# Attention values in plain float32 on two halves of the array, one burst per pair of units

## The chip, the core and the metric

The kernel runs on one core of a Trainium2 chip. The core has five engines that work through queues of their own, in order: TensorE (matmuls, written PE; its weight loads are written PEld), VectorE (DVE), ScalarE (ACT), GpSimd (POOL) and SyncE (SP, which issues most transfers). Matmuls write into PSUM, eight banks of 128 partitions by 2 KB; the other data lies in SBUF. The metric is the device time of the whole kernel in microseconds, as the median of several runs. Beside it there is one profiled execution, from which all rows in this document come; an instruction of the kernel is named there by its line (L1235).

## What is computed

One layer of a hybrid attention block for 128 prompt tokens (tile 0) and 1024 latent tokens (tiles 1 to 8 of 128 tokens), in float32. A modulated RMS norm is followed by one input projection, then by two groups of attention heads, each with 8 query heads, 2 key/value heads and 64 columns a head, by a SiLU gate, and by one output projection.

```python
def global_attn_latent(q, k_lat, v_lat, k_ctx, v_ctx):           # mixer A
    ...
        s = jnp.einsum('bqkgd,bskd->bkgqs', qblk, k_all).astype(jnp.float32) * (d ** -0.5)
        p = jax.nn.softmax(s, axis=-1).astype(v_all.dtype)
        return jnp.einsum('bkgqs,bskd->bqkgd', p, v_all)

def window_attn_latent(q, k_lat, v_lat, k_ctx, v_ctx, sink):     # mixer B
    ...
    s = jnp.concatenate([sink_column(sink, kv, s_ctx.shape[:-1]), s_ctx, s_band], axis=-1)
    p = jax.nn.softmax(s, axis=-1).astype(v_lat.dtype)
    ...

def merge_out(o_a, g_a, o_b, g_b, w_out):
    return jnp.concatenate([o_a * jax.nn.silu(g_a), o_b * jax.nn.silu(g_b)], axis=-1) @ w_out
```

Mixer A attends to all 1024 latent keys and 128 context keys, nine blocks of 128 keys. Mixer B attends to the context block and to a band of at most three latent blocks. The prompt tile attends to its own block alone.

## The kernel before, in words

Up to about 302 us the kernel makes the modulated activations, the queries, keys, values and gates. The change touches there only how V is put away. The rest is the attention part, and this document is about it.

**Units, slots and pairs.** A *unit* is one token tile, one mixer (`m` = 0 for A, 1 for B) and one key/value head, with its four query heads side by side as 512 columns. The units run in pairs: a unit of A, then the unit of B of the same tile and head. Latent units come first (32, in 16 pairs), then the prompt's four. A unit consists of *slots*, one for each block of keys: nine for A; four for B, three in the first and the last tile; a prompt unit has one slot and an empty one. So a pair has mostly 13 slots, which are numbered 0 to 12 here.

**A slot.** The main loop at the end of `hybrid_step` goes over all slots. Each round first calls `tick()`, which runs what was put off with `later(n, f)` to this round. Then come, in this order, `scores` of the slot, the maxima and mixer-B scores that are due (`due`), some output products from the list `outq`, and `values` of the slot that was `LAG` = 3 rounds earlier. `in_order` then fixes this order on every engine, so that a waiting instruction holds up all that was written after it on the same engine.

- `scores`, mixer A: two products give the transposed scores of 128 keys by 512 queries in a PSUM bank `st` (tag B, two banks). The second of them (L1218) brings in the shift by the row's maximum, through `qb`. ACT makes the exponential `pe` (L1220) and casts it to the reduced format (`ph`, L1221). GpSimd subtracts to get the remainder `pl` (L1225), in one block of nine DVE does (L1223).
- `scores`, mixer B: four transposes of weights that are computed with the queries as rows (`penat`, L1212), then `ph` and `pl` in the same way by ACT (L1213) and DVE (L1214).
- `values`: V is stored as `v_hi` (its reduced format, 64 columns, and 64 more columns that are ones for A and V's remainder for B) and `v_lo`. Products L1235 (`ph`), L1237 (`v_lo`, A only) and L1238 (`pl`) add up 64 rows of values and, for A, 64 rows that all hold the sum of the exponentials, in a bank `pv` (tag C, two banks).
- The end of a unit, put off by the numbers in `END_AT`, counted from its last `values`: `inverse` (ACT takes the inverse sum as the exponential of a negative logarithm, or copies the second 64 rows for B), `gated` (DVE, two halves, L1259; GpSimd multiplies by the gate `sgl`, L1261; `load_gate` fetches the gate of a unit further on), `parts` (ACT casts to `ogh`, L1271; GpSimd subtracts to get `ogl`, L1274, one round later) and, after a unit of B, 24 output products appended to `outq` (L1313). They are taken from there at 2.5 a round. The first two products use `ogh` of the pair's A unit, the third `ogl` of it.

**What runs beside it.** In slots 0 to 3 of a pair the mixer-B scores `sn` (L998, L999) are made; DVE takes their maximum (L1002), and ACT their exponential one round later (L988). In slot 4 `finish` puts `ex` on GpSimd (L1020), and two rounds later `sum` (L1034). The inverse of these sums goes through a transpose and two transfers, and GpSimd multiplies it into the B gate (L1045). The maxima of a later A unit (L941, read by DVE at L942) stand in slots 4, 5, 7 and 8 (seven of them) and 9 to 12 (five, of which two in slot 11). After the last one they are turned (`ptm`, L960, in slot 12), and DVE writes them into `qb` (L961), which the next pair's slot 0 reads. At the end of a tile's output products DVE does two operations on each half of 512 columns (L1318, L1319).

**Elsewhere.** `modulate_rows` (L375) and `gate_rows` (L651) use plain float32 products with weights of 32 columns, on quarters of the array beside each other.

Of the kernel before, what the change touches and what calls it, by code (L numbers as in the profile page):

```python
# [18 lines left out]
P = 128  # L19
# [17 lines left out]
LAG = 3  # L37
# [41 lines left out]
PES = 3  # L79
GATE_LATE = 2  # L80
END_AT = (1, 4, 6, 9)
PROMPT_END = (2, 4, 5, 7)
# [48 lines left out]
def hybrid_step(ctx, tc, x_prompt, x_sample, cache_k_a, cache_v_a, cache_k_b, cache_v_b,  # L131
# [631 lines left out]
    v_hi = kv.tile([P, 2, 20, 2, HD], F32R, name="v_hi")  # L763
    v_lo = kv.tile([P, 20, HD], F32R, name="v_lo")
# [7 lines left out]
    def split_values(src, j):  # L772

        nc.vector.tensor_tensor(v_lo[:, j : j + 2, :], src[:, 0], v_hi[:, 0, j : j + 2, 0, :], op=ALU.subtract)
        nc.vector.tensor_tensor(v_hi[:, 1, j : j + 2, 1, :], src[:, 1], v_hi[:, 1, j : j + 2, 0, :], op=ALU.subtract)

    with tc.tile_pool(name="kt", bufs=2) as kt:
        W_GB.pools[WRAW : WRAW + 2] = [(kt, 2)] * 2
        sg_tile.append(lambda n: kt.tile([P, 512], F32, tag="kh", name=n))
        for b in range(0, 20, 4):  # L780
            later(4 + b // 2, lambda b=b: nc.gpsimd.tensor_scalar(
                v_hi[:, 0, b : b + 4, 1, :], gain4, 0.0, 1.0, op0=ALU.mult, op1=ALU.add))
        ones = ident_r.bitcast(F32)[64:68].unsqueeze(1)
        for out, n in ((kla[64:68].rearrange("p g b n -> p (g b) n"), 18), (klp[64:68, 0:2], 2)):
            later(ONES_AT, lambda out=out, n=n: nc.vector.tensor_scalar(
                out, ones.to_broadcast([4, n, P]), 0.0, 1.0, op0=ALU.mult, op1=ALU.add))
# [94 lines left out]
        later(VC_AT, lambda: nc.scalar.copy(v_hi[:, :, 0:2, 0, :], vc))  # L881
        later(VC_AT + 1, lambda: split_values(vc, 0))
# [295 lines left out]
    def blocks(t, m, g):  # L1178

        if t == 0:  # L1180
            k = (khp[:, g, :], klp[0:68, g, :]) if m == 0 else 0
            return [(k, v_hi[:, m, 18 + g], v_lo[:, 18 + g, :])]
        if m == 0:
            return [((kha[:, g, b, :], kla[:, g, b, :]), v_hi[:, 0, 2 * b + g], v_lo[:, 2 * b + g, :]) for b in range(9)]
        p0, p1_ = window(t)
        at = {p: b + 1 for b, p in enumerate(POS)}
        return [(p - p0, v_hi[:, 1, 2 * at.get(p, 0) + g], None) for p in range(p0, p1_)]
# [5 lines left out]
    def load_gate(i):  # L1193
        if i < NU:
            t, m, g = units[i]
            sgl[i] = w2.tile([P, 2, P], F32, tag="sgl", name=f"sgl{i}")
# [4 lines left out]
    def parts_tiles(i, b):  # L1201
        return [w3.tile([P, 512], F32R, tag=n, name=f"{n}{i}_{b}") for n in ("ph", "pl")]

    def scores(i, b, blk):
# [3 lines left out]
        ph, pl = parts_tiles(i, b)  # L1208
        if m == 1:
# [9 lines left out]
        pe = w3.tile([P, 512], F32, tag="pe", name=f"pe{i}_{b}", bufs=PES)  # L1219
        nc.scalar.activation(pe, s, AF.Exp)  # L1220
        nc.scalar.copy(ph, pe)  # L1221
        if (i - PROMPT_AT in PROMPT_PL) if t == 0 else b in PL_DVE:
            later(1, lambda: nc.vector.tensor_tensor(pl, pe, ph, op=ALU.subtract))  # L1223
        else:
            nc.gpsimd.tensor_tensor(pl, pe, ph, op=ALU.subtract)  # L1225
        return ph, pl

    def values(i, b, last, blk, ph, pl):
        t, m, g = units[i]
        _, vh, vl = blk  # L1230
        if b == 0:
            pvb[i] = bank(PROMPT_PV[i - PROMPT_AT] if t == 0 else "C", f"pv{i}")
        pv = pvb[i]
        two = vh.rearrange("p s d -> p (s d)")
        nc.tensor.matmul(pv, two, ph, start=(b == 0), stop=False)  # L1235
        if m == 0:
            nc.tensor.matmul(pv[0:64, :], vl, ph, start=False, stop=False)  # L1237
        nc.tensor.matmul(pv, two, pl, start=False, stop=last)  # L1238
        if not last:
            return  # L1240
# [210 lines left out]
```

## Time and profile before

| | |
|---|---|
| runs, lowest / median / highest | 704.09 / 704.34 / 704.47 us |
| profiled execution, its span | 704.1 us |
| first score product of the attention part (L1217) | 301.85 us |
| transfers | 78.64 MB, mean 112 GB/s |

The page of the profile gives each engine's busy time and its share of the span, then groups of instructions as "line, engine, operation, written tile <- read tiles, shape, xcount | busy us, mean ns of one | idle us of the engine ahead of them, and what ended it". Lines of the order of time begin with start and duration in us. A line of the windows view has the stretch and its length, then the busy time of PE, PEld, DVE, ACT and POOL with their instruction counts, TensorE's granted clock, the share of the transfer engines and GB/s. `[0.43 <-PE st L1218]` says that the engine stood idle for 0.43 us until PE's write of `st` at that line. TensorE's clock is granted in full for nearly the whole span.

### The profile page before, as it was taken

The numbers are of one execution on the slowest core, as the hardware profiler recorded it, in microseconds if no ns is written. First come the engines' busy times: TensorE is split into PE (matmuls) and PEld (weight loads), VectorE is DVE, ScalarE is ACT, GpSimd is POOL, SyncE is SP. The second block draws the span as 40 slices with busy tenths as digits, with TensorE's granted clock in tenths as the row PEclk, the third lists the DMA queues.
The fourth block names the chain that finished last, engine by engine and source line by source line (L and its number), as shares of the span: only waits on it lengthen the run. The fifth ranks groups of instructions, "written<-read, shape, count | busy, mean of one in ns | idle before, by whom it ended". The sixth has DMA issues, their size and how long they took to land.

```text
span 704.1 us, 10711 instructions
## 1 busy us (share of the span) xinstructions
PE 691.6 (98%) x3554; PEld 561.4 (80%) x3554; DVE 443.3 (63%) x991; ACT 420.0 (60%) x856; POOL 342.3 (49%) x364
## 2 busy tenths in 40 slices
PE   6999999999999999999999999999999999999997
PEld 2788988878788789986788888878888888887876
DVE  3555247875676873537677577667666775775564
ACT  4455411412233553389877877787788778877870
POOL 3457023332323241657857655755574557456742
PEclk9999999999999999999999999999999999999999
DMA  8960283348435015423222122121211231212324
GB/s 330 415 245 16 109 305 76 72 93 295 131 89 175 1 61 187 157 64 102 90 69 83 34 82 73 46 82 58 86 61 52 69 90 46 83 52 90 91 60 144
DMA packets 53447, 78.64 MB, mean 112 GB/s; under 512 B 6848, under 2 KB 25728, under 8 KB 52368
## 3 DMA queue, kind: packets, MB, share of 16 engines
q1 hardware_dynamic: 45360, 66.28, 27.8%
q10 hardware_dynamic: 8032, 11.68, 6.2%
q8 instruction: 28, 0.46, 0.3%
q14 instruction: 27, 0.22, 0.1%
HBM read 58.72 MB, written 19.21 MB: 111 GB/s over the span
## 4 chain that ended last, share of the span: by engine, by line
PE 88%; ACT 4%; DMA 2%; DVE 2%; issue 2%; ACTq 1%; SPq 0%; POOL 0%; DVEq 0%; POOLq 0%
PE po L1313 14%; PE pv L1238 6%; PE pv L1235 6%; PE pmx L941 5%; PE st L1217 4%; PE pv L1237 4%; PE st L1218 4%; PE pq L279 4%; PE pq L280 4%; PE pq L278 4%; PE st L1212 4%; PE pg L292 3%; PE pg L293 3%; PE pg L288 3%; PE pk L279 2%; PE pk L280 2%
## 5 line engine op out<-in xcount | busy, mean ns | idle before, releaser
L1225 POOL TENSOR_TENSOR pl<-pe,ph 128x512 fp32r<-128x512 f32 x130 | 167.9, 1294 | 141.9 <-DVE nm L1002 67.5
L942 DVE TENSOR_REDUCE mx<-pmx 128x1 f32<-128x384 f32 x192 | 101.4, 553 | 57.3 <-PE pmx L941 56.2
L1220 ACT ACTIVATE pe<-st 128x512 f32<-128x512 f32 x146 | 86.7, 594 | 27.1 <-PE st L1218 26.4
L1221 ACT CAST ph<-pe 128x512 fp32r<-128x512 f32 x146 | 90.6, 621 | 4.8
L1238 PE MATMUL pv<-pl,v_hi 128*128 128x512 f32 x208 | 82.5, 397 | 0.3 <-POOL pl L1225 0.3
L1235 PE MATMUL pv<-ph,v_hi 128*128 128x512 f32 x208 | 82.6, 397 | 0.0
L197 POOL TENSOR_TENSOR rs_q<-ms_q,mhalf 128x8 f32<-128x8 f32 x18 | 34.8, 1931 | 80.7 <-DVE ms_q L195 80.7
L1313 PE MATMUL po<-wo,ogh 128*128 128x512 f32 (+1 forms) x224 | 73.1, 387 | 0.0
L1002 DVE CUSTOM_DVE_ANT_0 sn<-sn,mask,nsink 128x512 f32<-128x512 f32 (+1 forms) x64 | 46.4, 724 | 41.0 <-PE sn L999 38.6
L941 PE MATMUL pmx<-kha,qt 128*128 128x384 f32 x192 | 61.0, 363 | 0.5 <-ACT pen L988 0.3
L1217 PE MATMUL st<-qt,kha 128*128 128x512 f32 x144 | 57.9, 402 | 0.1
L1237 PE MATMUL pv<-ph,v_lo 128*64 128x512 f32 x146 | 57.6, 395 | 0.0
L1218 PE MATMUL st<-qb,kla 68*128 68x512 f32 x144 | 57.1, 397 | 0.0
L1238 PEld LDWEIGHTS pv<-pl,v_hi 128*128 128x128 f32 x208 | 39.2, 188 | 17.3 <-POOL pl L1225 0.7
L988 ACT ACTIVATE pen<-sn,nm 128x512 f32<-128x512 f32 (+2 forms) x72 | 44.9, 625 | 5.8 <-DVE nm L1015 2.7
L1213 ACT CAST ph<-st 128x512 fp32r<-128x512 f32 x62 | 36.4, 587 | 19.7 <-PE st L1212 19.4
L1313 PEld LDWEIGHTS po<-wo,ogh 128*128 128x128 f32 x224 | 41.0, 188 | 6.2 <-ACT ogh L1271 0.3
L1235 PEld LDWEIGHTS pv<-ph,v_hi 128*128 128x128 f32 x208 | 39.3, 189 | 7.0 <-issue 0.3
L1313 PE MATMUL po<-wo,ogl 128*128 128x512 f32 (+1 forms) x112 | 43.2, 386 | 0.0
L1214 DVE TENSOR_TENSOR pl<-st,ph 128x512 fp32r<-128x512 f32 x62 | 42.4, 685 | 1.2 <-ACT ph L1213 0.7
L675 ACT ACTIVATE sqq<-pq 128x512 f32<-128x512 f32 x18 | 10.8, 598 | 53.3 <-PE pq L280 13.8
L941 PEld LDWEIGHTS pmx<-kha,qt 128*128 128x128 f32 x192 | 35.5, 190 | 6.4 <-DVE mx L942 1.2
(238 smaller groups left out, 1701.3 us busy)
## 6 DMA issues: line engine op xcount, KB each, us to landing
qt<-qd SPq DMA_DIRECT2D x36, 256.0 KB
wm<-in_w_mod_ss_dram SPq DMA_DIRECT2D x8, 1024.0 KB
qd<-qo0q ACTq DMA_DIRECT2D x36, 128.0 KB
qd<-qo1q ACTq DMA_DIRECT2D x36, 128.0 KB
sgl<-gd SPq DMA_DIRECT2D x36, 128.0 KB
out_dram<-yt SPq DMA_DIRECT2D x17, 256.0 KB
xn<-in_x_sample_dram SPq DMA_DIRECT2D x8, 512.0 KB
wg<-in_w_mod_g_dram SPq DMA_DIRECT2D x4, 1024.0 KB
```

Source lines behind the costliest of these rows:

```text
L941: nc.tensor.matmul(pm[:, 0:384], lhs, kha[:, g, 3 * b : 3 * b + 3, :], start=True, stop=True)
L942: nc.vector.tensor_reduce(mx[:, h, b : b + 1], pm[:, 0:384], axis=AX.X, op=ALU.max)
L1002: nc.vector.tensor_tensor_reduce(s, s, mask[:, m0 : m0 + n], -1.0, nsink[:, 4 * g + h : 4 * g + h + 1], op0=ALU.add, op1=ALU.min, accum_ou ...
L1217: nc.tensor.matmul(s, kh, qtile[i], start=True, stop=False)
L1218: nc.tensor.matmul(s, kl, qbtile[i], start=False, stop=True)
L1220: nc.scalar.activation(pe, s, AF.Exp)
L1221: nc.scalar.copy(ph, pe)
L1225: nc.gpsimd.tensor_tensor(pl, pe, ph, op=ALU.subtract)
L1235: nc.tensor.matmul(pv, two, ph, start=(b == 0), stop=False)
L1237: nc.tensor.matmul(pv[0:64, :], vl, ph, start=False, stop=False)
L1238: nc.tensor.matmul(pv, two, pl, start=False, stop=last)
L1313: nc.tensor.matmul(po[c], x, wo_parts[KT * n + k][lo][:, q], start=(k == KS[0] and p == 0), stop=(k == KS[-1] and p == 2))
```

## The change

V is kept in plain float32 (`v_all`), not split, and the exponentials are not split either: `scores` leaves one tile `pe` (15 buffers of it). For A, GpSimd adds the nine exponential tiles of a unit into one, `acc`, as they come. `values` is no longer called slot by slot: two rounds after the last slot of a pair it is called for both of its units, one after the other, and makes all their products in one burst. Each block is two plain float32 products with 64 weight columns and 256 moving columns, one for the even and one for the odd heads, into PSUM partitions 0 to 63 and 64 to 127. For A, one more such step with a tile of ones gives the sums from `acc`. The end of a unit then works on 128 partitions by 256 columns. For A the inverse sums go into the gate by GpSimd, and DVE makes one product; for B the copy of the second half is gone. The delays become `ENDS`, gates are loaded four units ahead instead of two, and all `pv` are in tag C.

```diff
-LAG = 3
+LAG = 2
...
-PES = 3
+PES = 15
...
-END_AT = (1, 4, 6, 9)
-PROMPT_END = (2, 4, 5, 7)
+ENDS = ((1, 3, 4), (1, 2, 3, 6))
...
-    v_hi = kv.tile([P, 2, 20, 2, HD], F32R, name="v_hi")
-    v_lo = kv.tile([P, 20, HD], F32R, name="v_lo")
+    v_all = kv.tile([P, 2, 20, HD], F32, name="v_all")
+    ones = kv.tile([P, HD], F32, name="ones")
+    nc.gpsimd.memset(ones, 1.0)
...
         def put_values(src, t):
             j = 2 * t if t else 18
-            nc.scalar.copy(v_hi[:, :, j : j + 2, 0, :], src)
-            later(1, lambda: split_values(src, j))
+            nc.scalar.copy(v_all[:, :, j : j + 2, :], src)
...
     def scores(i, b, blk):
...
-        ph, pl = parts_tiles(i, b)
+        pe = w3.tile([P, 512], F32, tag="pe", name=f"pe{i}_{b}", bufs=PES)
         if m == 1:
...
-            nc.scalar.copy(ph, s)
-            later(1, lambda: nc.vector.tensor_tensor(pl, s, ph, op=ALU.subtract))
-            return ph, pl
+            nc.scalar.copy(pe, s)
+            return pe
...
         nc.scalar.activation(pe, s, AF.Exp)
-        nc.scalar.copy(ph, pe)
-        if (i - PROMPT_AT in PROMPT_PL) if t == 0 else b in PL_DVE:
-            later(1, lambda: nc.vector.tensor_tensor(pl, pe, ph, op=ALU.subtract))
+        if b == 0:
+            acc[i] = pe
         else:
-            nc.gpsimd.tensor_tensor(pl, pe, ph, op=ALU.subtract)
-        return ph, pl
+            first = acc[i]
+            if b == 1:
+                acc[i] = w3.tile([P, 512], F32, tag="acc", name=f"acc{i}", bufs=2)
+            nc.gpsimd.tensor_tensor(acc[i], first, pe, op=ALU.add)
+        return pe
...
-        nc.tensor.matmul(pv, two, ph, start=(b == 0), stop=False)
-        if m == 0:
-            nc.tensor.matmul(pv[0:64, :], vl, ph, start=False, stop=False)
-        nc.tensor.matmul(pv, two, pl, start=False, stop=last)
...
+        def product(o, lhs, rhs, start, stop):
+            r = rhs.rearrange("p (c s n) -> p c s n", s=2, n=P)
+            for s in range(2):
+                nc.tensor.matmul(pv[HD * s : HD * s + HD, o : o + 256].rearrange("p (c n) -> p c n", c=2), lhs,
+                                 r[:, :, s, :], start=start, stop=stop)
+
+        n = len(made)
+        for b, (blk, pe) in enumerate(made):
+            product(0, blk[1], pe, b == 0, m == 1 and b == n - 1)
         if m == 0:
+            product(256, ones, acc.pop(i), False, True)
...
         def inverse():
-            v["rs"] = w2.tile([64, 512], F32, tag="rs", name=f"rs{i}", bufs=1)
             if m == 1:
-                nc.scalar.copy(v["rs"], pv[64:128, :])
                 return
-            nc.scalar.activation(v["rs"], pv[64:128, :], AF.Ln)
-            nc.scalar.activation(v["rs"], v["rs"], AF.Exp, scale=-1.0)
+            rs = w2.tile([P, 256], F32, tag="rs", name=f"rs{i}")
+            nc.scalar.activation(rs, pv[:, 256:512], AF.Ln)
+            nc.scalar.activation(rs, rs, AF.Exp, scale=-1.0)
+            sg = sgl[i]
+            later(1, lambda: nc.gpsimd.tensor_tensor(sg, sg, rs.rearrange("p (c n) -> p c n", c=2), op=ALU.mult))
 
         def gated():
...
-            for s in range(2):
-                nc.vector.tensor_tensor(of[64 * s : 64 * s + 64], pvv[:, :, s, :], srv[:, :, s, :],
-                                        op=ALU.add if m else ALU.mult)
-            nc.gpsimd.tensor_tensor(of, of, sgl.pop(i), op=ALU.mult)
-            later(GATE_LATE, lambda: load_gate(i + 2))
+            nc.vector.tensor_tensor(of, pv[:, 0:256].rearrange("p (c n) -> p c n", c=2), sgl.pop(i), op=ALU.mult)
+            later(GATE_LATE, lambda: load_gate(i + 4))
...
-        ends = PROMPT_END if t == 0 else END_AT if i < PROMPT_AT - 2 else LAST_END
-        for n, f in zip(ends, (inverse, gated, parts)):
+        for n, f in zip(ENDS[m], (inverse, gated, parts)):
             later(n, f)
         if m == 1:
-            later(ends[3], lambda: outq.extend(out_items(t, g)))
+            later(ENDS[m][3], lambda: outq.extend(out_items(t, g)))
...
-        if s < len(slots):
-            live.append((slots[s], slots[s] and scores(slots[s][0], slots[s][1], slots[s][3])))
+        if s < len(slots) and slots[s]:
+            i, b, last, blk = slots[s]
+            live.setdefault(i, []).append((blk, scores(i, b, blk)))
+            if last and units[i][1] == 1:
+                ready[s + LAG] = i
...
-        if s >= LAG and live:
-            slot, parts = live.pop(0)
-            if slot:
-                values(*slot, *parts)
+        if s in ready:
+            i = ready.pop(s)
+            for j in (i - 1, i):
+                values(j, live.pop(j))
```

More of the change, by code (lines that the diff above doesn't have):

```diff
@@ L1361, in hybrid_step @@
     put(LATE_PUT + 3 * LATE_LAG + 3, load_adaln)
[L1362 to L1365 removed]
+    credit, live, ready = 0.0, {}, {}
+    for i in range(4):
+        load_gate(i)
+    for s in range(len(slots) + LAG + ENDS[1][3]):
         tick()
[L1367 to L1368 removed]
+        if s < len(slots) and slots[s]:
[3 more added lines that the diff above has]
+                ready[s + LAG] = i
         for n, at in WO_LATE.items():
```

47 lines of the change are left out of this document (13 added, 34 removed).

## The prediction

> **What bounds the kernel now.** I read the page's busy line first, then its groups, then a steady stretch of the attention part by windows, then single instructions in order of time.
>
> ```profile
> span 704.1 us, 10711 instructions
> ...
> PE 691.6 (98%) x3554; PEld 561.4 (80%) x3554; DVE 443.3 (63%) x991; ACT 420.0 (60%) x856; POOL 342.3 (49%) x364
> ...
> L1221 ACT CAST ph<-pe 128x512 fp32r<-128x512 f32 x146 | 90.6, 621 | 4.8
> L1238 PE MATMUL pv<-pl,v_hi 128*128 128x512 f32 x208 | 82.5, 397 | 0.3 <-POOL pl L1225 0.3
> ```
>
> TensorE is the bound and stands still for nobody: 0.3 us of idle time ahead of 208 products. The mean of 397 ns is no price, because matmuls overlap; the price is the distance from start to start. The windows view of 413.04 to 603.95 us (all engines; then L998 alone, which a pair of units runs four times) and lines of the order of time give it:
>
> ```profile
> 413.04:603.95 190.91, 190.91 (x921) 153.51 (x921) 131.75 (x281) 149.84 (x297) 112.70 (x120) 1.00 0.21 67
> 413.04:603.95 190.91, 12.59 (x32) 6.08 (x32) 1.00 0.21 67
> 499.77 0.39 PE L1235 MATMUL pv<-ph,v_hi 128*128 128x512 f32 x1
> 500.00 0.39 PE L1237 MATMUL pv<-ph,v_lo 128*64 128x512 f32 x1
> 500.23 0.40 PE L1238 MATMUL pv<-pl,v_hi 128*128 128x512 f32 x1
> 500.46 0.40 PE L1217 MATMUL st<-qt,kha 128*128 128x512 f32 x1
> 500.70 0.40 PE L1218 MATMUL st<-qb,kla 68*128 68x512 f32 x1
> 500.94 0.51 PE L941 MATMUL pmx<-kha,qt 128*128 128x384 f32 x2
> 501.14 0.60 ACT L1220 ACTIVATE pe<-st 128x512 f32<-128x512 f32 x1 [0.43 <-PE st L1218]
> 501.28 0.39 PE L1235 MATMUL pv<-ph,v_hi 128*128 128x512 f32 x1
> ```
>
> 32 products of L998 are 8 pairs, so a pair (9 score blocks of mixer A, mostly 4 of mixer B: 13 slots) takes 23.9 us, all of it TensorE. The order of the busy columns is PE, weight loads, DVE, ACT, POOL: per pair DVE has 16.5 us of work, ACT 18.7, POOL 14.1, and all of it is hidden. A product of 512 columns costs 0.235 us, one of 384 (L941) 0.17, and its reader starts 0.44 us after it (500.70 to 501.14).
>
> **The change, part by part.** *Values, before:* 9 x 3 + 4 x 2 = 35 products, 35 x 0.235 = 8.2 us a pair.
>
> *Values, after:* 13 blocks and one product with the ones are 14 steps, each of two plain float32 products of 256 columns, on the two halves of the array. The kernel already has plain float32 products on quarters of the array (L651: 32 columns wide, 512 moving):
>
> ```profile
> 155.08 0.39 PE L280 MATMUL pq<-whiqb,h 128*128 128x512 f32 x1
> 155.39 0.16 PEld L651 LDWEIGHTS pgate<-wg,sil32g 128*32 128x32 f32 x8 [0.35 <-issue]
> 155.40 0.64 PE L651 MATMUL pgate<-wg,sil32g 128*32 128x512 f32 x4
> 155.85 1.04 PE L651 MATMUL pgate<-wg,sil32g 128*32 128x512 f32 x8
> 156.28 1.04 PE L651 MATMUL pgate<-wg,sil32g 128*32 128x512 f32 x8
> 156.71 0.61 PE L651 MATMUL pgate<-wg,sil32g 128*32 128x512 f32 x4
> 157.25 0.44 PE L703 MATMUL ptq<-ident_r,qfq 128*128 128x128 f32 x2
> 47.47 0.50 PE L292 MATMUL pg_f<-h,whiga 128*128 128x512 f32 x1
> 47.81 0.39 PE L293 MATMUL pg_f<-h,wloga 128*128 128x512 f32 x1
> ```
>
> Eight products in the source (one call of `gate_rows`) leave 16 records, two for each, in rounds of four that start at 155.40, 155.85, 156.28 and 156.71 (the rows come from neighbouring windows and overlap): four quarters run side by side, and a round of 512 columns takes 0.43 us, so one of 256 takes 0.215. I take the same for two halves: two rounds, 0.43 us a step, 14 x 0.43 = 6.0 us a pair. The upper bound is no overlap of the halves, 0.86 a step; the lower one is this price, since the rounds are as long with four tiles as a pass over the columns asks.
>
> *Entering and leaving the halves.* Into L651, 155.08 to 155.40 is 0.32 where 0.235 is usual: 0.09 lost. Out of it, 156.71 + 0.43 = 157.14, but L703 starts at 157.25: 0.11 lost. After the other such group L292 to L293 takes 0.34: 0.1 more. I take 0.3 us a burst. L1237 (64 columns, at the array's first column) stands 0.23 from both its full-width neighbours, so the lower bound is 0. The Trainium skill (TensorEngine Tiling (Array Packing), section Tiling Modes) says that changing the mode, and not merely the tile, drains the engine. L651 agrees, L1237 does not; going by L1237 the sum would be 16 x 0.3 = 5 us lower.
>
> TensorE's own work so falls by 8.2 - 6.3 = **1.9 us a pair**, 30.4 us over 16 pairs. The two prompt pairs go from 5 x 0.235 = 1.2 to 3 x 0.43 + 0.3 = 1.6 us: +0.9 in all.
>
> *Edits that I cost at nothing.* The 146 casts (L1221), the remainders of mixer B on DVE, the copies of the sums and the splitting of V go from engines that TensorE hides; ACT comes to 18.7 - 9 x 0.62 - 1 = 12 us a pair. `load_gate` issues the same 36 DMAs two units earlier, into four buffers, and on the SP queue they pass only loads that are needed later. Uncovered they could cost a landing, which nothing waits for as long as a whole pair lies between.
>
> *What GpSimd does now.* 128 adds instead of 130 subtractions of the same size. But the order matters. From a pair's last value product to its first output product there were 9 slots and are now 6, and the burst is a stretch in which TensorE makes nothing for the others. When it ends (call that 0) TensorE begins slot 2 of the next pair, and GpSimd's queue then holds: add 2, gate x inverse sums, add 3, add 4, `ex`, `ol` of B, add 5, `sum`, `ol` of A. The third output product, in slot 8, waits for this last one, and behind it on TensorE stand all later scores. Prices from start to start:
>
> ```profile
> 488.66 1.28 POOL L1225 TENSOR_TENSOR pl<-pe,ph 128x512 fp32r<-128x512 f32 x1 [0.70 <-ACT ph L1221]
> 489.91 0.73 POOL L1045 TENSOR_TENSOR sgl<-sgl,spare 128x256 f32<-128x256 f32 x1
> 490.61 0.73 POOL L1261 TENSOR_TENSOR spare<-spare,sgl 128x256 f32<-128x256 f32 x1
> 494.82 0.20 POOL L1020 TENSOR_TENSOR ex<-nm,sink 128x4 f32<-128x4 f32 x1
> 494.97 0.74 POOL L1274 TENSOR_TENSOR ogl<-spare,ogh 128x256 fp32r<-128x256 f32 x1
> ```
>
> A 512-wide operation is 1.25 (488.66 to 489.91), a 256-wide one 0.70, `ex` and `sum` 0.15 each, the last `ol` to its end 0.74: 4 x 1.25 + 0.70 + 0.15 + 0.70 + 0.15 + 0.74 = 7.4 us. Add 2 starts once its exponential is there, 0.235 + 0.44 + 0.60 and a hand-over: 1.35 us. ACT adds a wait, because it has the mixer-B exponentials of slots 2 and 3 between its own:
>
> ```profile
> L1002 DVE CUSTOM_DVE_ANT_0 sn<-sn,mask,nsink 128x512 f32<-128x512 f32 (+1 forms) x64 | 46.4, 724 | 41.0 <-PE sn L999 38.6
> L988 ACT ACTIVATE pen<-sn,nm 128x512 f32<-128x512 f32 (+2 forms) x72 | 44.9, 625 | 5.8 <-DVE nm L1015 2.7
> ```
>
> Slot 2's second `sn` starts at 0.70, DVE has it 0.44 later and is done at about 2.0; then ACT has L988, an exponential, a 256-wide cast, L988 and the exponential for add 4, about 0.65 + 0.55 + 0.35 + 0.65 + 0.6: 4.8, where GpSimd would be free at 1.35 + 1.25 + 0.70 + 1.25 = 4.55. With 0.3 more for this and the hand-overs, `ol` of A is there at **9.1 us**. TensorE's own work up to there is 14 score products, 4 of `sn`, 7 output products (25 x 0.235) and 7 maxima (0.17): 7.0 us. **It waits 2.1 us**, in 15 pairs. Bounds: 0 (a queue 2.1 us shorter) and 3.2 (ACT later by the casts and exponentials of slots 5 and 6, 1.1).
>
> *The shifted maxima (`qb`).* Without the values, slots 9 to 12 are only some 1.2 us long. DVE has the two maxima of slot 11, in every second pair two output operations, then `qb`, which the second score product of slot 0 needs:
>
> ```profile
> 501.31 1.02 DVE L942 TENSOR_REDUCE mx<-pmx 128x1 f32<-128x384 f32 x2 [0.96 <-PE pmx L941]
> 530.59 0.60 PE L1212 MATMUL st<-ident_r,pen 128*128 128x128 f32 x4
> 530.79 0.68 DVE L961 TENSOR_TENSOR qb<-ptm,diag 4x512 fp32r<-4x512 f32 x1 [0.36 <-PE ptm L960]
> 530.94 0.42 PE L941 MATMUL pmx<-kha,qt 128*128 128x384 f32 x1
> L1319 DVE TENSOR_TENSOR yt<-po,yt 128x512 f32<-128x512 f32 x17 | 11.8, 691 | 0.6
> ```
>
> From slot 11's first maximum product: 0.4 to DVE's start (500.94 to 501.31), 1.0 for two maxima, 1.3 for two output operations, 0.7 for `qb`: 3.4 us. TensorE is there after two maxima 0.35, two output products 0.47, transposes 0.35 and the small one before them 0.06, a maximum 0.17, three output products and one score product 0.94: 2.3. That is 1 us in every second pair, say 0.45 on average (bounds 0 and 1).
>
> *Ends.* After each of these waits the weights load late, 0.1 us as at L293: 3 us in all. In pair 1 no output products fill slots 2 and 3: 1.2 us more. At the end
>
> ```profile
> 679.61 1.34 issue
> 680.98 1.55 POOL pl L1225
> 684.47 15.87 PE po L1313 x92
> ```
>
> the chain's wait for the prompt's `pl` (up to 2.9 us) goes; its values then wait for one exponential. I count -1.5.
>
> *Sum:* -30.4 + 0.9 + 15 x (2.1 + 0.45) + 3 + 1.2 - 1.5 = **+11.5 us**. The profiled span is 704.1 and the median of the runs 704.34: I forecast **716 us**.
>
> **The rivals.** *A. GpSimd's queue holds nothing up* (faster). Were an add well under 1 us, or the slots longer than I think, the saving stays: 704.3 - 30.4 + 0.9 + 7 + 1.5 (restarts) - 1.5 = 682 us, and 677 without the switch. For it: POOL has only 14.1 us of work in 23.9; against it: its order is fixed, and 1.25 us an add. It decides where the 9.1 us fall to 7.0; at 8.3 the kernel stands even.
>
> *B. The halves don't overlap* (slower): 226 steps at 0.86 instead of 0.43 add 97 us, 813. Against it: the rounds of four in L651. The Trainium skill (TensorE: Matmul & The Clock Gate, Part 3, The mechanism) says that weight loads overlap running products only where their row groups differ, and both halves use all rows. L651's eight loads, four of them for the next round, disagree: they share their rows and are done within 0.16 us of 155.39, ahead of the round that needs them.
>
> *C. The sums come late* (slower): the product with the ones waits for add 8. After 9.1 us come three more adds, 12.9 us; the next such product stands at about 22. It decides once an add takes twice 1.25; at 2 us a pair more, 746.
>
> **How the numbers follow.** My case 0.51, A 0.34, B 0.08, C 0.04, and 0.03 for no change that the measurement could tell (within 0.2%, 1.4 us, where my case and A meet). Slower: 0.51 + 0.08 + 0.04 = 0.63; faster 0.34; same 0.03. My case spans 706 to 738: waits of 1.5 to 3.2 and `qb` between 0.4 and 0.9. The range goes down to 680, which takes in nearly all of A and leaves out B and C.
>
> **What would show it.** Right: steps of 0.43 us in bursts of some 6.3 us; a pair of 24.4 to 24.9 us; output products that wait about 2 us for `ogl` by POOL, and score products for `qb` by DVE. Wrong: no POOL releaser ahead of the output products and a pair near 22.3 us (A); steps of 0.86 us (B); products with the ones that wait for POOL (C).

## The result and the profile after

| | before | after |
|---|---|---|
| runs, median (lowest to highest) | 704.26 us (704.09 to 704.47, 4 runs) | 730.30 us (726.96 to 731.52, 4 runs) |
| ratio of the times, 95% interval | | 1.0361 (1.0336 to 1.0386) |
| profiled execution, its span | 704.1 us | 729.5 us (its time 731.25 us) |

The change makes the kernel 26 us slower, where 11.7 were forecast. First the page of the changed kernel: its span, the engines' busy line, and three of its groups (L1225 is a value product, L931 the product whose maximum VectorE takes, called a transposed maximum below, L1300 an output product; L1262, which ends waits in the last, is the subtraction that makes `ogl`).

```profile
span 729.5 us, 10886 instructions
...
PE 688.9 (94%) x3896; PEld 526.7 (72%) x3896; DVE 378.2 (52%) x857; ACT 311.8 (43%) x692; POOL 323.2 (44%) x340
...
L1225 PE MATMUL pv<-pe,v_all 128*64 128x256 f32 x832 | 96.8, 381 | 0.0
L931 PE MATMUL pmx<-kha,qt 128*128 128x384 f32 x192 | 66.5, 388 | 11.1 <-DVE mx L932 5.6
L1300 PE MATMUL po<-wo,ogl 128*128 128x512 f32 (+1 forms) x112 | 46.1, 412 | 9.7 <-POOL ogl L1262 9.6
```

ScalarE went from 420 to 312 us and VectorE from 443 to 378, and the kernel is slower: both were hidden before. TensorE's share fell from 98% to 94%. The span grew by 25 us, and what stands behind TensorE is to be read from its waits. The windows view divides the attention part (the columns are as before):

```profile
299.95:315.25 15.30, 13.37 (x71) 11.02 (x70) 6.43 (x15) 11.83 (x26) 10.12 (x10) 1.00 0.30 86
315.25:340.77 25.52, 23.45 (x118) 16.99 (x117) 12.81 (x30) 11.79 (x28) 16.52 (x18) 0.80 0.33 99
340.77:667.11 326.34, 303.40 (x1756) 214.92 (x1755) 161.33 (x359) 156.31 (x353) 175.73 (x185) 1.00 0.21 64
667.11:692.98 25.87, 24.39 (x134) 17.93 (x133) 8.95 (x21) 11.69 (x31) 13.40 (x16) 0.87 0.28 89
692.98:729.47 36.49, 31.68 (x206) 24.45 (x204) 12.82 (x27) 9.34 (x31) 6.63 (x11) 1.00 0.25 83
442.92:645.05 202.13, 188.25 (x1090) 133.24 (x1088) 100.54 (x225) 96.21 (x216) 106.05 (x112) 1.00 0.21 63
```

The rows are pair 0, pair 1, pairs 2 to 14, pair 15, and the prompt's units with the last output; the last row is 8 steady pairs, 25.27 us each (23.87 before). By starts of score products, before against after: start of the attention part 301.85 and 299.95, pair 0 18.46 and 15.30, pair 1 20.43 and 25.52, pairs 2 to 14 308.11 and 326.34, pair 15 22.41 and 25.86, the rest 32.83 and 36.49. So 18.2 of the 25.4 us come in the steady pairs and 7.2 net at the two ends. That pair 0 is shorter and the prompt's stretch longer belongs together: a pair's burst now falls into the next stretch.

The chain that ended last, from one burst to the third output product of the next pair (start us, us, what):

```profile
496.62 6.20 PE pv L1225 x56
502.81 0.43 PE st L1205
...
504.09 0.76 DVE sn L992
...
504.94 0.78 ACT pen L978 x2
505.72 0.49 ACT pe L1207
506.21 0.29 ACT ogh L1259
506.50 0.68 ACT pen L978 x2
507.19 0.50 ACT pe L1207
...
507.82 0.70 POOL acc L1214
...
509.25 0.69 POOL ogl L1262
...
511.29 0.74 POOL ogl L1262
...
512.07 0.96 PE po L1300 x3
```

Between the first score product after the burst and the third output product the path leaves TensorE: it runs through VectorE's maximum, ScalarE's five operations and GpSimd's queue to A's `ogl`. In the order of time the two ends of that stretch are:

```profile
502.75 0.51 PE L1205 MATMUL st<-qt,kha 128*128 128x512 f32 x1
512.07 0.50 PE L1300 MATMUL po<-wo,ogl 128*128 128x512 f32 x1 [0.96 <-POOL ogl L1262]
```

That is 9.32 us, and TensorE's own work in it is 14 score products, 4 `sn`, 6 output products and 7 maxima: 24 x 0.235 + 7 x 0.17 = 6.8 us. The row's 0.96 us is only what is left of the 2.5 us of waiting when TensorE reaches it; the rest was spent in small waits on the way. In the text below "the stretch" is this one.

Outside it, in every second pair, VectorE is late with `qb` (order of time, VectorE and TensorE):

```profile
466.60 0.69 DVE L1305 TENSOR_TENSOR po<-po,spare 128x512 f32<-128x512 f32 x1
467.33 0.69 DVE L1306 TENSOR_TENSOR yt<-po,yt 128x512 f32<-128x512 f32 x1
468.05 0.68 DVE L951 TENSOR_TENSOR qb<-ptm,diag 4x512 fp32r<-4x512 f32 x1
468.79 0.50 PE L1206 MATMUL st<-qb,kla 68*128 68x512 f32 x1 [0.67 <-DVE qb L951]
```

Two operations on a finished output half stand ahead of `qb`. So the pairs alternate between 24.80 and 25.73 us.

### The profile page after: what moved, and what is told of

Same layout as the page of the kernel before. It is cut to its first block, busy times and chain, and to the rows that moved or that the text cites. A ratio compares the mean times of both kernels' runs of the same rounds, so it can differ in the third digit from the quotient of the medians.

```text
span 729.5 us, 10886 instructions
## 1 busy us (share of the span) xinstructions
PE 688.9 (94%) x3896; PEld 526.7 (72%) x3896; DVE 378.2 (52%) x857; ACT 311.8 (43%) x692; POOL 323.2 (44%) x340
## 4 chain that ended last, share of the span: by engine, by line
PE 72%; ACT 7%; POOL 6%; DVE 6%; issue 5%; DMA 3%; ACTq 1%; SPq 0%; DVEq 0%; POOLq 0%
PE pv L1225 14%; PE po L1300 11%; PE pq L278 4%; PE pq L279 4%; PE pq L277 4%; PE st L1201 3%; ACT pen L978 3%; PE pg L287 3%; PE pg L291 3%; PE pg L292 3%; POOL ogl L1262 3%; POOL acc L1214 2%; PE pmx L931 2%; ACT pe L1207 2%; PE pk L278 2%
## 5 line engine op out<-in xcount | busy, mean ns | idle before, releaser
L1214 POOL TENSOR_TENSOR acc<-acc,pe 128x512 f32<-128x512 f32 x112 | 143.6, 1282 | 88.5 <-ACT pe L1207 84.8
L1225 PE MATMUL pv<-pe,v_all 128*64 128x256 f32 x832 | 96.8, 381 | 0.0
L1225 PEld LDWEIGHTS pv<-pe,v_all 128*64 128x64 f32 x832 | 58.2, 137 | 33.7 <-issue 6.0
L931 PE MATMUL pmx<-kha,qt 128*128 128x384 f32 x192 | 66.5, 388 | 11.1 <-DVE mx L932 5.6
L1300 PE MATMUL po<-wo,ogh 128*128 128x512 f32 (+1 forms) x224 | 75.6, 398 | 0.0
L1202 ACT COPY pe<-st 128x512 f32<-128x512 f32 x62 | 36.4, 587 | 55.9 <-PE st L1201 55.9
L978 ACT ACTIVATE pen<-sn,nm 128x512 f32<-128x512 f32 (+2 forms) x72 | 45.3, 631 | 28.4 <-DVE nm L992 25.4
L1214 POOL TENSOR_TENSOR acc<-pe,pe 128x512 f32<-128x512 f32 x16 | 20.4, 1276 | 82.8 <-ACT pe L1207 82.8
L1300 PE MATMUL po<-wo,ogl 128*128 128x512 f32 (+1 forms) x112 | 46.1, 412 | 9.7 <-POOL ogl L1262 9.6
L931 PEld LDWEIGHTS pmx<-kha,qt 128*128 128x128 f32 x192 | 35.8, 195 | 25.0 <-ACT pen L978 12.1
L1300 PEld LDWEIGHTS po<-wo,ogh 128*128 128x128 f32 x224 | 42.6, 195 | 3.8
L1205 PEld LDWEIGHTS st<-qt,kha 128*128 128x128 f32 x144 | 27.5, 191 | 24.0 <-ACT pe L1207 14.5
L1201 PE MATMUL st<-ident_r,pen 128*128 128x128 f32 x248 | 38.5, 279 | 1.1 <-ACT rs L1240 1.1
L440 POOL TENSOR_TENSOR h<-hf,h 128x256 fp32r<-128x256 f32 (+2 forms) x33 | 28.0, 863 | 20.6 <-DVE h L439 20.6
L1201 PEld LDWEIGHTS st<-ident_r,pen 128*128 128x128 f32 x248 | 30.1, 144 | 8.1 <-ACT ogh L1259 1.5
L1206 PEld LDWEIGHTS st<-qb,kla 68*128 68x128 f32 x144 | 27.8, 193 | 9.9 <-DVE qb L951 6.7
```

What stands on the lines that cost most here:

```text
L931: nc.tensor.matmul(pm[:, 0:384], lhs, kha[:, g, 3 * b : 3 * b + 3, :], start=True, stop=True)
L978: nc.scalar.activation(penat[i][:, h], s, AF.Exp, bias=v["nm"][:, h : h + 1], scale=scale, accum_out=v["sum"][:, h : h + 1])
L1201: nc.tensor.transpose(s[:, P * h : P * h + P], penat[i][:, h, o : o + P], ident_r.bitcast(F32))
L1205: nc.tensor.matmul(s, kh, qtile[i], start=True, stop=False)
L1206: nc.tensor.matmul(s, kl, qbtile[i], start=False, stop=True)
L1214: nc.gpsimd.tensor_tensor(acc[i], first, pe, op=ALU.add)
```

## The experiments

All are edits of the changed kernel; line numbers stay within a few of its own. Pair means the steady pairs of the profiled execution, and ratios are to the kernel before.

**Is it A's remainder in GpSimd's queue?** Three edits reach it in three ways. First, the output products of a pair are begun one slot later:

```diff
-ENDS = ((1, 3, 4), (1, 2, 3, 6))
+ENDS = ((1, 3, 4), (1, 2, 3, 7))
```

> Only change: a pair's 24 output products enter the list one slot later (slot 8 instead of 7). Theory Q (TensorE waits for GpSimd's queue: the third output product needs the A unit's remainder, which is there 9.25 us after the burst): the third product then stands in slot 9, behind work that ends later than that, so that wait goes; a pair falls from 25.3 to 23.2 to 24.2 us and the kernel to 700 to 715. Rival S (the slots after the burst are simply too short for ScalarE and VectorE; the output product only shows the wait that comes last): the wait moves to the score products and the kernel stays above 722.

704.93 us, ratio 1.0010 (0.9997 to 1.0023), pair 23.42 us. One slot number takes back all of the loss. The stretch is 9.50 us long now, but a whole slot more of TensorE's work lies in it, 8.1 us in place of 6.8, and TensorE no longer stands idle ahead of the third product.

Second, the queue is shortened. This kernel leaves out the adds of blocks 2 to 8, so its sums are those of two blocks:

```diff
             if b == 1:
                 acc[i] = w3.tile([P, 512], F32, tag="acc", name=f"acc{i}", bufs=2)
-            nc.gpsimd.tensor_tensor(acc[i], first, pe, op=ALU.add)
+                nc.gpsimd.tensor_tensor(acc[i], first, pe, op=ALU.add)
```

> Leaves out the adds of blocks 2 to 8 (the sums are those of two blocks), so GpSimd has seven operations of 1.25 us fewer a pair, three of them ahead of the A remainder. Theory Q: the remainder is there some 5.5 us after the burst, before TensorE comes to it; its wait is gone and the waits for banks and for the maxima stay: a pair of 24.0 to 24.4 us, 708 to 716 in all. Rival S: at most 3 us better than the changed kernel.

704.83 us, ratio 1.0009 (1.0000 to 1.0019), pairs of 23.43 and 24.98 us. The stretch shrinks to 8.08 and 8.68 us only, still over the 6.8 us of TensorE's work. Its third output product, in the order of time, has no wait in front of it any more:

```profile
449.50 0.40 PE L1300 MATMUL po<-wo,ogl 128*128 128x512 f32 x1
```

So GpSimd's queue is worth 0.6 to 1.2 us of the stretch. The other 1.3 to 1.9 us over TensorE's work are waits ahead of that product, at transposed maxima and score products, for ScalarE and VectorE.

Third, the same work in another order, A's end ahead of B's:

```diff
-ENDS = ((1, 3, 4), (1, 2, 3, 6))
+ENDS = ((1, 2, 3), (1, 3, 4, 6))
...
-            later(1, lambda: nc.gpsimd.tensor_tensor(sg, sg, rs.rearrange("p (c n) -> p c n", c=2), op=ALU.mult))
+            nc.gpsimd.tensor_tensor(sg, sg, rs.rearrange("p (c n) -> p c n", c=2), op=ALU.mult)
```

> The same work in another order: the A unit's end comes one slot before the B unit's, and GpSimd multiplies the gate by the inverse sums at once, before add 2. No operation is added or removed. Theory Q: the remainder of A then stands behind adds 2 to 4 and ex only, about 6 us after the burst, and nothing waits for it; the B remainder is needed only by the ninth output product. 24.0 us a pair, 706 to 716 in all. Rival S: within 3 us of the changed kernel, for all engines have the same work.

708.92 us, ratio 1.0070 (1.0053 to 1.0088), pairs of 23.57 and 24.86 us, a stretch of 8.20 and 8.57 us. All three came within what was expected of them or, the second, a little below, and all say that GpSimd's queue sets the end of the stretch in the changed kernel: in the steady pairs of none of them does TensorE stand idle for `ogl`. They don't explain the alternation, which stays in the second and the third.

**Is the burst worth it, and do the halves overlap?** Without the burst, each block's products two slots after its scores as before, with the sums one slot after A's last block:

```diff
...
-            for j in (i - 1, i):
-                values(j, live.pop(j))
+        if s in todo:
+            i, b, pe, blk = todo.pop(s)
+            values(i, "block", b, pe, blk, len(blocks(*units[i])))
+        if s in ended:
+            values(ended.pop(s), "end")
```

> The burst is undone: each block's two plain float32 products run two slots after its scores, the product with the ones one slot after the last of A. TensorE goes into and out of the halves 14 times a pair instead of once. Theory Q with a switch of 0.33 us (as the burst's two ends show): 4.3 us of switches more and about 3 us of waits less, 25.5 to 27 us a pair, 733 to 755. Rival S with a switch that costs nothing (as L1237 showed before): about 22.4 us a pair, 685 to 695.

739.26 us, ratio 1.0494 (1.0478 to 1.0510), pair 25.94 us, as expected. One step between full-width products, in the order of time (L1304 is the output product here, L1229 the value product):

```profile
500.38 0.62 PE L1304 MATMUL po<-wo,ogh 128*128 128x512 f32 x2
500.93 0.65 PE L1229 MATMUL pv<-pe,v_all 128*64 128x256 f32 x4
501.52 0.50 PE L1205 MATMUL st<-qt,kha 128*128 128x512 f32 x1
501.86 0.40 PE L1206 MATMUL st<-qb,kla 68*128 68x512 f32 x1
```

Two output products take 0.55 in place of 0.47, the step 0.59 in place of 0.43, the score product behind it 0.34 in place of 0.235: 0.08 + 0.16 + 0.10 = 0.34 us for entering and leaving, 14 times a pair.

Then one burst for each unit, not for each pair:

```diff
-            if last and units[i][1] == 1:
-                ready[s + LAG] = i
+            if last:
+                ready[s + LAG + (units[i][1] == 0)] = i
...
-            for j in (i - 1, i):
-                values(j, live.pop(j))
+            values(i, live.pop(i))
```

> Edit: one burst per unit and not per pair: A's products follow three slots after A's last block, B's two slots after B's last. One burst more, so one more switch of about 0.33 us a pair; A's remainder comes some nine slots earlier and nothing of A is in GpSimd's queue behind B's burst. Theory of two causes: the 1.0 us at the third output product goes, 0.3 comes, and the 1.5 us at the maxima and `qb` stay: a pair of 24.3 to 24.8 us, 713 to 722 us. Rival (the slots behind A's burst are B's, whose four transposes and copies are short, so TensorE runs into ScalarE there): a pair of 25.3 us or more, 729 or more.

709.18 us, ratio 1.0077 (1.0057 to 1.0096), pair 23.69 us: the wait for A's remainder goes, as said, but the pair gains 1.6 us where 0.5 to 1.0 were expected. Why more, was not followed up.

Last, the burst's products in another order:

```diff
...
-        for b, (blk, pe) in enumerate(made):
-            product(0, blk[1], pe, b == 0, m == 1 and b == n - 1)
-        if m == 0:
-            product(256, ones, acc.pop(i), False, True)
+        for s in range(2):
+            for b, (blk, pe) in enumerate(made):
+                product(s, 0, blk[1], pe, b == 0, m == 1 and b == n - 1)
+            if m == 0:
+                product(s, 256, ones, acc[i], False, True)
```

> Edit: the same 28 products of a burst in another order: all of one half of the array's columns, then all of the other, for each unit. If two products take 0.43 us together only because neighbours stand on different halves, a product alone takes 0.43 us, the burst grows from 6.2 us by 10 to 12 products, 4.3 to 5.2 us, the other engines get that much rest, which takes up to 1.3 us of the 4.2 us of waits, and a pair is 28.3 to 30.5 us: 778 to 815 us. Rival (a product of 256 columns costs 0.22 us wherever it stands, and the halves side by side give nothing): a pair of 25.1 to 25.4 us, 728 to 733 us.

786.88 us, ratio 1.1170 (1.1156 to 1.1185), pairs of 28.4 and 29.4 us. The burst in the chain that ended last, and its first records in the order of time (two records a product; L1224 is the value product here):

```profile
461.91 9.81 PE pv L1224 x56
...
461.83 4.16 PE L1224 MATMUL pv<-pe,v_all 128*64 128x256 f32 x20
```

Time and pair are within what was expected of halves that overlap. The burst takes 9.81 us for 6.20. Where one half alone is at work the records stand 0.216 us apart, so a product takes 0.43 us, as much as two on different halves take together. The burst grew by 3.6 us, less than the 4.3 to 5.2 that were expected, because the next half begins before the last products of the one ahead (two of the 20 records are the next half's).

**Is the rest VectorE?** Moving `qb` alone a slot forward:

```diff
-MX_LEAD = 3
+MX_LEAD = 4
```

> Edit: the maxima of the next unit are finished (`m4`, `mnat`, and from there `qb`) one slot earlier, nothing else. If the wait at `qb` (1.5 us in every second pair) is a term of its own, as the prediction has it: it goes, the pair is 24.4 to 25.0 us on average, 715 to 727 us. Rival: the last of the transposed maxima, which then stand closer to the reduction, are late in its place; the pair stays at 25.1 to 25.4 us, 728 to 732.

726.68 us, ratio 1.0311 (1.0293 to 1.0329), pair 24.98 us without alternation: 0.3 of the 0.47 us that the alternation costs on average. Then the two operations that stand ahead of `qb` are left out (for the latent tokens; what is stored is `x`):

```diff
-                nc.vector.tensor_tensor(po[c], po[c], gt[n][:, q], op=ALU.mult)
-                nc.vector.tensor_tensor(yt[n][:, q], po[c], yt[n][:, q], op=ALU.add)
+                if last:
+                    nc.vector.tensor_tensor(po[c], po[c], gt[n][:, q], op=ALU.mult)
+                    nc.vector.tensor_tensor(yt[n][:, q], po[c], yt[n][:, q], op=ALU.add)
```

> Edit on the changed kernel: leaves out VectorE's two operations on a finished output half (times the gate, plus `x`) for all tokens but the prompt's, so what is stored there is `x` alone; no product is left out and none is moved. If the waits at the transposed maxima and at `qb` in every second pair come from these operations standing ahead in VectorE's queue, they go, as with 2.2 products a slot (23.87): a pair of 23.7 to 24.3 us, 704 to 716 us. Rival (the rate helped because TensorE's own products came in another order): the pair stays at 24.9 to 25.3 us, 722 to 731 us.

722.89 us, ratio 1.0271 (1.0254 to 1.0288), pair 24.80 us in place of 23.7 to 24.3: my theory missed. These operations are worth 0.47 us a pair and no more. The wait at a transposed maximum in the long pairs, 0.79 us by VectorE, is gone too without these operations. But it lies inside the stretch, whose length is 9.33 us in both kernels, within 0.01. A wait that a longer chain covers costs nothing. The ends of the stretch, first in a long pair of the changed kernel (with that wait), then in the kernel without the operations:

```profile
477.94 0.51 PE L1205 MATMUL st<-qt,kha 128*128 128x512 f32 x1
...
483.68 0.44 PE L931 MATMUL pmx<-kha,qt 128*128 128x384 f32 x1 [0.79 <-DVE mx L932]
...
487.28 0.50 PE L1300 MATMUL po<-wo,ogl 128*128 128x512 f32 x1 [0.49 <-POOL ogl L1262]
```

```profile
473.26 0.50 PE L1205 MATMUL st<-qt,kha 128*128 128x512 f32 x1
482.59 0.50 PE L1300 MATMUL po<-wo,ogl 128*128 128x512 f32 x1 [0.96 <-POOL ogl L1262]
```

**The rate of the output products.** One number, in three sizes:

```diff
-OUTRATE = 2.5
+OUTRATE = 2.2
```

> Edit: the products of the output projection are handed out at 2.2 a slot and not 2.5, nothing else. The steady pair of the changed kernel is 25.27 us on average, 21.1 of work and 4.2 of waits; about 1.0 of these stands at the third output product (A's remainder, in GpSimd's queue) and about 1.5 at the transposed maxima and at `qb`, in every second pair alone (VectorE's queue, where the two operations on a finished output half come just ahead of them). Theory of two causes: the third product stays in the slot where it was, so its 1.0 us stays, but the finished half comes about a slot later and no longer falls ahead of the maxima and `qb`: a pair of 23.7 to 24.4 us without the alternation, 703 to 716 us. Rival (all of it hangs on A's remainder, and the rest of the waits follows it): a pair of 25.0 to 25.3 us, 725 to 731.

713.26 us, ratio 1.0133 (1.0097 to 1.0169), pair 23.87 us without alternation, as expected. That was luck in part: the reason given for it, VectorE's operations out of the way, is worth 0.47 of the 1.40 us, as the run without them shows. The other two sizes, 2.67 and 2.0, and 2.2 in the kernel without VectorE's operations:

> Edit on the changed kernel: the output products at 2.67 a slot and not 2.5, so the 24 of a pair stand in 9 slots (10 at 2.5, 11 at 2.2), and four slots of 13 have none. The wait of 1.4 us a pair that 2.2 takes away, of which VectorE's output operations account for 0.47 us alone, is then put to two theories. Empty slots: a slot without output products holds 0.6 to 0.8 us of TensorE's work and meets ScalarE at its limit (busy without a gap in slots 4 and 5), so each further empty slot costs about what the last one did, 0.5 to 1.2 us: a pair of 25.8 to 26.5 us, 737 to 749 us. Rival (the step from 2.5 to 2.2 is VectorE's operations falling somewhere else, which could go either way): within 0.4 us of 25.27, or below, 723 to 737 us.

> Edit on the changed kernel: the output products at 2.0 a slot, in 12 slots of 13, one empty. Empty slots: the one taken away (slot 5) had about 0.8 us of work against ScalarE's full occupation; where there is little idle time left, the gain is small: a pair of 23.2 to 23.8 us (23.87 at 2.2), 702 to 713 us. Rival (VectorE's operations fall at another place): 24.0 us or more, 716 or more.

> Edit: the run that leaves out VectorE's two operations on an output half (24.80 us a pair, 722.9 us) with the products at 2.2 a slot. If the rate alone already took VectorE's collision away (0.47 us of its 1.4), leaving the operations out brings nothing more: a pair of 23.75 to 23.95 us, 707 to 713 us, and the rest of the rate's gain, 0.93 us, is TensorE's own products filling a slot. If the two are apart: 23.3 to 23.5 us, 699 to 706 us.

| products a slot | us, ratio (interval) | pair, us | stretch, us | of these own work | output products in it |
|---|---|---|---|---|---|
| 2.67 | 736.48, 1.0460 (1.0444 to 1.0475) | 24.93 / 26.65 | 9.48 / 10.23 | 6.6 | 5 |
| 2.5 | 730.30, 1.0361 (1.0336 to 1.0386) | 24.80 / 25.73 | 9.32 | 6.8 | 6 |
| 2.5, no VectorE operations | 722.89, 1.0271 (1.0254 to 1.0288) | 24.80 | 9.32 | 6.8 | 6 |
| 2.2 | 713.26, 1.0133 (1.0097 to 1.0169) | 23.87 | 9.32 | 7.5 | 9 |
| 2.2, no VectorE operations | 713.29, 1.0134 (1.0117 to 1.0151) | 23.86 | 9.32 | 7.5 | 9 |
| 2.0 | 710.98, 1.0098 (1.0076 to 1.0119) | 23.87 | 9.32 | 7.8 | 10 |

The stretch keeps its length within 0.02 us while six to ten output products lie in it; with five, at 2.67, it is longer, and why was not followed up. Three products more inside cost nothing there, and are 3 x 0.235 = 0.7 us less outside. By that account this is most of the 0.93 us that 2.2 gains beyond VectorE's 0.47. The 0.47 lies within the rate's effect: with VectorE's operations gone, 2.2 gives the same pair. The account is not complete, for the tenth product at 2.0 is free inside as well, but the pair does not become shorter by it. Two of the free products, at 2.2 a slot, and the end of the stretch:

```profile
444.05 0.51 PE L1205 MATMUL st<-qt,kha 128*128 128x512 f32 x1
...
447.81 0.39 PE L1300 MATMUL po<-wo_big,ogh 128*128 128x512 f32 x1
448.05 0.39 PE L1300 MATMUL po<-wo_big,ogl 128*128 128x512 f32 x1
...
453.37 0.50 PE L1300 MATMUL po<-wo,ogl 128*128 128x512 f32 x1 [0.95 <-POOL ogl L1262]
```

At 2.67 the pair is at the lower edge of what was expected (25.79 on average), but the time, 736.48 us, lies just below its range and within the rival's. At 2.0 the pair gains nothing over 2.2 where a small gain was expected. That ScalarE is what slows TensorE in the slots without output products, as those expectations have it, was read from the chain above; no run takes ScalarE's work alone out of it, and the one edit meant for it (B's end one slot earlier) gave no time. It is not shown.

**Both together.** A's end first, and 2.2 a slot:

> Edit: A's end before B's with the gate product at once (as in the run of that order, 708.9 us, pairs of 23.57 and 24.86) and the output products at 2.2 a slot. Two causes that add: the remainder's wait is gone by the order, the waits at the maxima and at `qb` in every second pair by the rate: pairs of 22.4 to 23.0 us, so 708.9 less 15 times 1.2 to 1.8: 682 to 692 us, faster than the kernel before. Rival (one cause, which the order alone already took): pairs stay at 24.0 to 24.3 us, 705 to 710.

**691.07 us, ratio 0.9813 (0.9798 to 0.9828)**, as expected, and faster than both kernels, than the one before by 1.9%. Order and rate add: 25.27 us a pair, 24.22 with the order, 23.87 with the rate, 22.77 with both, where the sum of the two gains gives 22.82. Its page and two of its windows, pair 1 and eight steady pairs:

```profile
span 688.3 us, 10869 instructions
...
PE 671.3 (98%) x3896; PEld 522.7 (76%) x3896; DVE 377.1 (55%) x857; ACT 309.7 (45%) x692; POOL 323.7 (47%) x340
```

```profile
315.15:336.25 21.10, 19.48 (x116) 13.30 (x116) 12.19 (x30) 11.73 (x29) 16.60 (x18) 1.00 0.38 119
427.90:610.06 182.16, 181.60 (x1089) 134.48 (x1088) 99.84 (x225) 95.04 (x217) 106.50 (x112) 1.00 0.22 70
```

The same engines do the same work as in the changed kernel (377 for 378 us on VectorE, 323.7 for 323.2 on GpSimd), and TensorE stands at 98% again. Two further attempts, the first with one burst for each unit and 2.2 a slot, the second from the run at 691:

> Edit: one burst per unit (709.2 us, pairs of 23.69) and the output products at 2.2 a slot. If a second burst takes the same wait away as the order does (A's remainder) and the rate takes VectorE's, the two add as order and rate did (25.27 to 22.74): a pair of 22.5 to 23.1 us, 692 to 701 us. Rival (the extra burst has already spaced out what VectorE has to do): 23.4 to 23.8 us, 705 to 711.

704.99 us, ratio 1.0011 (0.9996 to 1.0025), pair 23.20 us: a little above the range, and the time further above it, since pairs 1 and 15 of the profiled execution (24.88 and 26.76 us, 21.11 and 21.59 in the run at 691) keep their waits.

```diff
-EX_AT = (2, 2, 5)
+EX_AT = (3, 3, 6)
```

> Edit: the run at 691.1 us (A's end first, 2.2 products a slot) with the sinks' short operations on ScalarE, GpSimd and VectorE (`ex`, `sum`, `inv`) one slot later. Its pairs are 22.63 and 22.85 us, 21.13 of them work. If what is left (1.6 us: transposes behind the last exponential of B 0.6, third product 0.1, first score products of a slot 0.5, `qb` 0.3) is ScalarE's pace, one slot more or less for these moves it little: 22.5 to 22.9 us, 688 to 693 us. Rival (these small operations stand in the way of the adds on GpSimd): 22.0 to 22.4, 680 to 687.

711.87 us, ratio 1.0102 (1.0089 to 1.0115), pair 23.69 us: both expectations missed. The stretch is as before (8.07 and 8.41 us), and the maxima behind it wait 0.70 us a pair for VectorE. The waits left over are not ScalarE's pace alone; one slot for three short operations undoes 0.92 us a pair.

## Why the forecast was too small

| term, us | forecast | measured |
|---|---|---|
| TensorE's own work with the switch, a pair | -1.9 | -1.9 |
| the stretch: chain, own work, wait | 9.1, 7.0, 2.1 | 9.3, 6.8, 2.5 |
| `qb` | 0.45 | 0.47 |
| other waits and restarts, a pair | 0.2 | 0.3 |
| a steady pair, sum | 0.85 | 1.40 |
| pairs 2 to 14 | 11 | 18.2 |
| start, pairs 0, 1 and 15, prompt's units | 0.5 | 7.2 |
| sum | 11.5 | 25.4 |

(Own work: 35 products of 0.235 us are 8.2 us before; the burst takes 6.20 us to the next score product, and the product behind that comes 0.1 us late. The other waits are what the rest leaves of 1.40 us.)

*TensorE's own work, switch and halves: right.* Steps of 0.43 us (14 of them, with the way in, in 6.20 us), 0.34 us for a switch where 0.3 was taken. Rival B is answered by the products in turn: 0.43 us for a product alone, 0.43 us for one on each half. By the Trainium skill's rule (TensorE: Matmul & The Clock Gate, Part 3, The mechanism), weight loads overlap running products only where their row groups differ. The trace does not agree: the halves share their rows and still run side by side.

*GpSimd's queue: right in kind, and the chain nearly in size.* The queue stands in the trace in the order that the forecast gave (add 4, `ex`, `ol` of B, add 5, `sum`, `ol` of A). The wait of 2.5 us is within its bounds (0 to 3.2). It is 0.4 us over the forecast because the chain is 0.2 longer and TensorE has six output products in it, where the forecast counted seven. What the forecast had at nothing is what lies under this wait: with the adds gone the stretch is not the 7.0 us of TensorE's work but 8.1 to 8.7. So rival A's 682 us did not come either where its condition was met: the run without the adds has no wait for `ogl` and takes 704.83. At 8.3, the forecast said, the kernel stands even; A's end first gave 8.2 and 8.6, and 1.007.

*Rival C* did not come: no wait for the sums is seen at the product with the ones.

*The step that failed is the ends.* They were counted at +1.2 for pair 1 and -1.5 for the tail, net some +0.5 with all that lies outside the steady pairs, and were 7.2. The forecast gave pairs 1 and 15 the waits of a steady pair, and pair 1 the missing output products besides. The path that it did not have goes from GpSimd through VectorE to ScalarE. In a steady pair GpSimd multiplies the inverse sums into B's gate (L1035) early in the burst, at 498.11 in the pair above. In pairs 1 and 15 this stands behind an add after the burst; VectorE's product with the gate (L1249) waits for it, the maximum of `sn` stands behind that in VectorE's queue, and ScalarE's `pen` and TensorE wait for the maximum. The chain that ended last, in pair 15, and then TensorE in pair 1 in the order of time:

```profile
677.30 1.28 POOL acc L1214
678.59 0.70 POOL sgl L1035
...
679.32 0.04 DVE spare L1249
...
679.66 0.42 DVE sn L992
...
680.37 0.67 ACT pen L978 x2
```

```profile
328.15 1.01 PE L931 MATMUL pmx<-kha,qt 128*128 128x384 f32 x2 [1.38 <-ACT pen L978]
```

The runs show that GpSimd's queue is the cause: without the adds all that lies outside pairs 2 to 14 is 2.5 us shorter than before instead of 7.2 longer, with A's end first it is 1.2 us longer, and with order and rate both put right it is 1.7 us shorter. Pairs 1 and 15, 51.4 us in the changed kernel, take 42.7 in the last of these.

Part of the 7.2 us comes with TensorE's clock, which the forecast left out altogether. In the changed kernel, windows of 3.4 us in pair 1:

```profile
324.40:327.80 3.40, 2.00 (x8) 0.88 (x6) 1.81 (x7) 1.94 (x5) 3.40 (x4) 1.00 0.00 0
327.80:331.20 3.40, 3.05 (x8) 2.63 (x9) 1.35 (x3) 2.56 (x8) 2.92 (x5) 0.50 0.77 232
331.20:334.60 3.40, 3.07 (x8) 2.18 (x8) 2.04 (x4) 0.90 (x2) 3.32 (x5) 0.50 0.35 120
334.60:338.00 3.40, 3.40 (x12) 2.62 (x12) 2.50 (x5) 0.59 (x1) 2.18 (x2) 0.50 0.00 0
338.00:341.40 3.40, 3.40 (x22) 2.98 (x21) 2.26 (x4) 1.92 (x4) 0.00 (x0) 0.99 0.00 1
```

Behind a window in which TensorE is busy for 2.00 of 3.40 us, at the waits for `pen`, the clock falls to one half, and stays there for 10 us. A second spell lies in pair 15 (0.87 in its window above). The four runs of this kernel had clocks of 0.988, 0.988, 0.991 and 0.996 and took 731.3, 731.5, 729.4 and 727.0 us: at the 0.997 of the profiled execution before, by an estimate from these four, some 4 us of the 26 would be gone. In the run at 691 us both windows are at 1.00.

*The steady pair* came 0.55 us a pair higher than forecast, 0.4 of it in the wait of the stretch and the rest in small waits. Over 13 pairs this is 7 us, the other half of the miss.

Besides these costs the forecast overlooked a lever: it took TensorE's place in the schedule as given. Its stretch of 7.0 us of work under 9.1 us of chain was a hole of 2.1 us, into which work can be moved. Output products of the last pair could be, and three more were at 2.2 a slot.

## What to carry to other kernels

When work is gathered into a burst, the slots that it leaves behind become shorter, and every delay that was counted in slots becomes shorter with them: count these again in microseconds along the chain that they wait for. Where such a chain is longer than the bound engine's work, move work into the hole before shortening the chain; and before a wait in a profile is mended, see whether it lies inside a longer one. Two small edits (A's end first, 2.2 for 2.5) turned 1.036 into 0.981 here.

## What the runs showed of the hardware

The clock of TensorE halved without a long pause: the longest single wait, at the start of the spell, was 1.38 us, TensorE had been busy for 2.00 of the last 3.40 us, and spells at half clock lasted 3.4, 6.8 or 10.2 us in the runs of this case, which are multiples of one length. The Trainium skill (TensorE: Matmul & The Clock Gate, Part 1: The HAM clock gate) lets the clock go after about 3.4 us of idleness; the length agrees, the idleness does not.

Two float32 products of 256 columns on different halves of the array take together what one takes alone, 0.43 us.
